# Transposing a branch's normed outputs on VectorE and through DRAM instead of on TensorE

## Chip, cores and metric

The kernel runs on one core of one Trainium2 chip. The metric is device time in microseconds (us) of one execution.

## What is computed

The reference is one layer of a decoder for 256 tokens of 2048 channels. Both of its branches read one input projection.

```python
def hybrid_mixer(h, w_in, ...):
    z = h @ w_in                       # one combined projection
    # A: gated delta rule, 8 heads of 128: o = gated_delta_rule(q, k, v, beta, g)
    oa = rms_norm(o, gdn_norm_w) * silu(zg)
    # B: block-sparse attention, 8 heads of 128 (256 tokens are one causal block)
    ob = moba_attention(mq, mk, mv) * silu(zm)
    y = sigmoid(ga) * (oa @ w_branch_a) + sigmoid(gb) * (ob @ w_branch_b)
    return y @ w_out
```

Only the part on `oa` is changed: its way from the normed and gated outputs (tokens on the partitions) to the operand of `oa @ w_branch_a` (channels on the partitions).

## The kernel before

**Precision.** Every large product is made of fp32r halves. `split` (L249 to L258) takes a block of weights as it came from DRAM (`raw_x`): ScalarE casts the upper half `hi_x` (L256), VectorE subtracts to get the lower half `lo_x` (L257). TensorE multiplies hi by hi, hi by lo and lo by hi. Weights of the input projection come in reads of 1 MB, two for a product; each read is split in two pieces of 128x1024, so that a product has the pieces `x_0_0`, `x_0_1`, `x_1_0`, `x_1_1`. There are three buffers for such a pair (`wspl`), and from some point a fourth, so a cast waits until TensorE has left an earlier piece.

**Order.** TensorE's instructions are pinned in program order by `mm` (L166) and `tr` (L169). Other engines' instructions get their places by a scheduler of the framework, except where `pin` (L164) fixes one. The large products follow the list `ORDER` (L47): `q0 mv0 zg0 q1 kq2 kq3 zg1 v0 v1 v2 ga0 zm0 zm1 mv1 v3 mk0 mk1 mk2 mk3 ga1 ga2 ua0 ua1`, then what is written behind it. Of these `mk3` is the last pair of attention heads (its query product `mq`, then its key product `mk`), `ga1` the next projection, `ua0` and `ua1` the branch products that need what is changed here. Small work is written as Python generators in queues (`gq`, `vq`, `mq`, `aq`, `bq`, `sq`, `zq` and others). `tick` (L159) advances each queue after a step of a large product; the numbers that a generator yields are the ticks that it waits.

**The delta rule's end.** `solve` (L1058) makes the outputs of 8 heads for two halves of 128 tokens. `normed` (L1075) normalizes and gates half `t` into an SBUF tile `oz_t` (128 tokens x 1024 channels, L1106). `prepare` (L876) then starts three 1 MB reads of branch weights on POOL's queue (`tq_g` twice, `tq_z` once, L862) and gives VectorE four sums of them (L870, 128x1024 each) and POOL one more read that accumulates (L873).

**The turn and its sums.** After all heads were attended, `turned_outputs` (L1122) transposes 16 tiles of 128x128 on TensorE (L1130) into four PSUM tiles `ot`; the list `held` stops the queues of the solver and of attention while it runs. `halved` (L1118) reads a PSUM tile twice with the norm's weight `gn` as scale: ScalarE writes the upper half of `oaT`, VectorE the lower. Then four sums of the quarters of `oa` are made, which the seven-product scheme of the branch product (`seven`, L916, a Strassen-like scheme) needs beside the quarters. They are made in PSUM, with copies of one operand to SBUF (`oa_f`) by ScalarE ahead, and halved into `oas`.

**The way through DRAM.** `moved` (L778) writes 32x32 blocks, which VectorE has transposed inside (STREAM_TRANSPOSE), to DRAM (L783) and reads them back in another order (L784), which completes a transpose. It serves attention's probabilities (`pT_d`, 384 KB, written on ScalarE's DMA queue) and the gates (`zm_d`, 256 KB, `turned_gate`, L1253, written on POOL's queue). Reads are on POOL's queue.

**Attention around the change.** `attention` (L1262) makes `mq` and `mk` of two heads; `halves` (L528) adds the two column halves of each head's product into `y_mk`: ScalarE copies one (L531), VectorE adds the other (L532); then VectorE multiplies by `rrow` (L1269). `attend` (L1190) waits for that.

Of the kernel before, what the change touches and what calls it, by code (L numbers as in the profile page):

```python
# [8 lines left out]
F32 = mybir.dt.float32  # L9
F32R = mybir.dt.float32r  # L10
BF16 = mybir.dt.bfloat16
AF = mybir.ActivationFunctionType
ALU = mybir.AluOpType
AX = mybir.AxisListType

P = 128
# [23 lines left out]
A_WAIT2 = 1.5  # L40
A_WAIT3 = 5
A_WAIT4 = 1
G_WAIT = (4, 5)

# [48 lines left out]
def hybrid_layer(  # L95
# [15 lines left out]
    nc = tc.nc  # L111
# [35 lines left out]
    def aux_tile(name):  # L147
        return aux.tile([P, 512], F32, tag="aux", name=name)
# [5 lines left out]

    extra = []

    held = []

    def tick():  # L159
        after[0] -= 0.5  # L160
        for q in (gq, vq, mq, *(() if held else (aq, bq)), *extra):
            q.tick()

    pin = tc.keep_in_program_order  # L164
# [4 lines left out]
    def tr(*args):  # L169
        return pin(nc.tensor.transpose(*args))  # L170
# [608 lines left out]
    def moved(blocks, back, name, writer=nc.gpsimd):  # L779

        n = blocks.shape[1] // 4
        d = dram.tile([4, P, n], F32, name=f"{name}_d")
        pin(writer.dma_start(d.rearrange("i (r j) x -> (i r) (j x)", j=4), blocks))  # L783
        pin(nc.gpsimd.dma_start(back.rearrange("p (i x) -> p i x", i=4), d.rearrange("i k x -> k i x")))  # L784
# [70 lines left out]
    def block(w, c, h, x):  # L855

        return w[h * 512 : (h + 1) * 512, (c + x) * 512 : (c + x + 1) * 512].rearrange("(k p) c -> p k c", p=P)

    def fetch(tq, w, c, order):

        for i in order:
            nc.gpsimd.dma_start(tq[i], block(w, c, *((0, 0), (1, 1), (0, 1))[i]))  # L862

    def weight_sums(tq, w, c, wait):

# [192 lines left out]
    def solve():  # L1058
        oT = big.tile([P, H, 2 * S], F32R, tag="u1", name="oaT")
        oaT[0] = oT  # L1060
        def step(t, which):
            for g in range(2):
                ps = aux_tile(f"sv_{t}_{which}_{g}")
                p3 = ps.rearrange("p (h e) -> p h e", e=P)
                for hh in range(4):
                    h = g * 4 + hh
                    o_ = slice(hh * P, (hh + 1) * P)
                    w = inv[t][:, h, :] if which == 0 else sl(h)[:, P : 2 * P]
                    mm(ps[:, o_], w, vt(0 if which else t, h), start=True, stop=True)
                if which == 0:  # L1070
                    nc.scalar.copy(gvt[g][:, t], p3)
                else:
                    nc.vector.tensor_tensor(gvt[g][:, 1], gvt[g][:, 1], p3, op=ALU.subtract)

        def normed(t, oz):  # L1075

            pso = [aux_tile(f"so_{t}_{g}") for g in range(2)]
            for g, ps in enumerate(pso):
                for hh in range(4):
                    h = g * 4 + hh  # L1080
                    o_ = slice(hh * P, (hh + 1) * P)
                    if t == 0:
                        mm(ps[:, o_], sl(h)[:, 2 * P : 3 * P], vt(0, h), start=True, stop=True)
                    else:
                        mm(ps[:, o_], sl(h)[:, 3 * P : 4 * P], vt(0, h), start=True, stop=False)
                        mm(ps[:, o_], sl(h)[:, 5 * P : 6 * P], vt(1, h), start=False, stop=True)
            for g, ps in enumerate(pso):
                for hh in range(4):
                    h = g * 4 + hh
                    jq = wk.tile([P, P], BF16, tag="jq", name=f"jo_{t}_{h}")  # L1090
                    nc.scalar.activation(
                        jq, ps[:, hh * P : (hh + 1) * P], AF.Square, accum_out=ssoo[:, t, h : h + 1]
                    )
                yield 0.5
            nc.vector.tensor_scalar(
                fo[:, t, :], ssq[:, t, :], EPS, EPS * P, op0=ALU.add, op1=ALU.mult
            )
            nc.vector.scalar_tensor_tensor(
                fo[:, t, :], ssoo[:, t, :], 1.0 / P, fo[:, t, :], op0=ALU.mult, op1=ALU.add
            )  # L1100
            nc.scalar.activation(fo[:, t, :], fo[:, t, :], AF.Sqrt)
            nc.vector.reciprocal(fo[:, t, :], fo[:, t, :])
            for g in range(2):
                for hh in range(4):
                    h = g * 4 + hh
                    nc.vector.scalar_tensor_tensor(  # L1106
                        oz[:, g, hh, :],
                        pso[g][:, hh * P : (hh + 1) * P],
                        fo[:, t, h : h + 1],
                        zg()[:, t, h * P : (h + 1) * P],  # L1110
                        op0=ALU.mult,
                        op1=ALU.mult,
                    )
                yield 0.5

        gn = pcol[:, NTAP * NCV : NTAP * NCV + 1]

        def halved(hi, lo, p3):  # L1118
            nc.scalar.activation(hi, p3, AF.Copy, scale=gn)
            nc.vector.scalar_tensor_tensor(lo, p3, gn, hi.bitcast(F32), op0=ALU.mult, op1=ALU.subtract)  # L1120

        def turned_outputs(ozs):  # L1122


            a = {}
            for t in (1, 0):
                for g in range(2):
                    pt = aux_tile(f"ot_{t}_{g}")
                    for hh in range(4):
                        tr(pt[:, hh * P : (hh + 1) * P], ozs[t][:, g, hh, :], ident)  # L1130
                    a[t, g] = pt.rearrange("p (h n) -> p h n", n=P)
            for t in (1, 0):
                for g in range(2):
                    ks = slice(4 * g, 4 * g + 4)
                    halved(oT[:, ks, t * P : (t + 1) * P], oT[:, ks, S + t * P : S + (t + 1) * P], a[t, g])
                yield 1
            oa_f = big.tile([P, 2, 4, P], F32, tag="tv", name="oa_f")
            x, y = (oa_f[:, i] for i in range(2))
            nc.scalar.copy(x, a[1, 1])
            nc.vector.tensor_tensor(a[1, 1], a[1, 0], x, op=ALU.subtract)  # L1140
            nc.scalar.copy(y, a[0, 0])
            nc.vector.tensor_tensor(a[0, 0], a[1, 1], y, op=ALU.subtract)
            nc.scalar.copy(x, a[0, 0])
            yield 1
            nc.vector.tensor_tensor(a[0, 1], a[0, 1], x, op=ALU.add)
            nc.vector.tensor_tensor(a[1, 0], y, a[1, 0], op=ALU.subtract)
            yield 1
            sums = [None] * 4
            for i, o, tag in ((0, (1, 1), "tt"), (1, (0, 0), "tw"), (3, (0, 1), None), (2, (1, 0), "tv")):
                if tag:  # L1150
                    tl = big.tile([P, 2, 4, P], F32R, tag=tag, name=f"oas_{i}")
                    sums[i] = tl[:, 0], tl[:, 1]
                else:
                    sums[i] = [wk.tile([P, 4, P], F32R, tag="s", name=f"oas_{i}_{n}") for n in ("hi", "lo")]
                halved(*sums[i], a[o])
                yield 1
            oas.extend(sums)

        while vq.items or v_left[0]:
            yield 1  # L1160
        for t, which in ((0, 0), (0, 1), (1, 0)):
            step(t, which)
            yield SV_WAIT
        ozs = [big.tile([P, 2, HG, P], F32, tag=tg, name=f"oz_{t}") for t, tg in enumerate(("tv", "tw"))]
        for t in range(NT):
            yield from normed(t, ozs[t])

        obs.append(big.tile([P, H, 2 * S], F32R, tag="g0", name="obT"))
        tg = big.tile([P, 2, 4, 512], F32, tag="g1", name="tq_g")
        tz = big.tile([P, 4, 512], F32, tag="z2", name="tq_z")  # L1170
        tq = tg[:, 0], tg[:, 1], tz
        prepare(tq, wa, 0, (0, 2, 1))
        yield OS_WAIT
        while attended[0] < H:
            yield 0.5
        held.append(True)
        yield from turned_outputs(ozs)
        held.pop()

    mv = big.tile([P, NT, GW], F32, tag="z1", name="mv")  # L1180

    def attention_values(c):
        pts = proj_n(w_in, CMV + c * 512, hT, KT, f"mv{c}")
        for t in range(NT):
            nc.scalar.activation(mv[:, t, c * 512 : (c + 1) * 512], pts[t], AF.Copy, scale=rstd[:, t : t + 1])


    attended = [0]
# [62 lines left out]
    extra.append(zq)  # L1251

    def turned_gate(p):  # L1253
        yield G_WAIT[p > 0]
        blocks = ga_[:, 2, p % 2]
        to = blocks.rearrange("p (i m t r) -> p t m i r", i=4, m=2, t=NT)
        x = zm()[:, p]
        for t in range(NT):
            pin(nc.vector.transpose(to[:, t], x[:, t].rearrange("p (m c i) -> p m i c", m=2, i=4)))
        moved(blocks, x.rearrange("p t x -> p (t x)"), f"zm_{p}")  # L1260
# [303 lines left out]
```

## Time and profile before

| | |
|---|---|
| median of 3 runs | 758.12 us (757.39 to 758.29) |
| profiled execution, its own time | 757.3 us |
| its span in the trace | 755.6 us |
| mean granted TensorE clock | 0.997 of full speed |
| bytes read from and written to DRAM | 166.39 MB, 6.82 MB |

The profile is of one execution. Its span runs from the first to the last recorded instruction, its own time is 1.7 us longer. PE is TensorE's matrix products, PEld its weight loads (beside the products), DVE VectorE, ACT ScalarE, POOL GpSimd, SP SyncE. A transpose on TensorE is listed as a MATMUL by `ident`. Matrix products overlap: each is listed with its whole duration of 0.4 us, while the next starts 0.23 us later. What a step costs TensorE is therefore read from the distance of starts. Busy times of an engine add up its instructions; an idle time in brackets stands ahead of the instruction that ended it, with what released it.

### The profile page before, as it was taken

Reading aid. Unit: us, or ns where it says so; the run is one execution under the profiler, and the core shown is the slowest. Engines: PE = TensorE matmul, PEld = TensorE weight load, DVE = VectorE, ACT = ScalarE, POOL = GpSimd, SP = SyncE. Lnnn points to the kernel's source line nnn. Section 1 sums busy time; section 2 is a strip of 40 time slices with the busy share of each in tenths; the row PEclk is TensorE's granted clock in tenths of the full one; section 3 lists DMA queues with packets and bytes.
Section 4 is the critical chain, followed back from the end, with each engine's and each line's share of the span. In section 5 each row is a group of like instructions: output and inputs, shape, how many; then the busy total and the mean of one; then the engine's idle time right before and its main releaser. Section 6 shows DMA issues by size and latency. Waiting matters only on the chain.

```text
span 755.6 us, 10416 instructions
## 1 busy us (share of the span) xinstructions
PE 746.3 (99%) x3858; PEld 636.6 (84%) x3858; DVE 597.6 (79%) x963; ACT 456.0 (60%) x693; POOL 65.3 (9%) x97
## 2 busy tenths in 40 slices
PE   9999999999999999999999999999999999999996
PEld 7898988899888888888998888887888888888885
DVE  6877779986988999877568886788796778789864
ACT  6776666667655655455556485557555655765741
POOL 1000201112000000022011100101000101000000
PEclk9999999999999999999999999999999999999998
DMA  9586576458676657698267975998988887987862
GB/s 303 187 259 204 171 234 181 139 149 247 199 248 199 204 182 207 180 273 282 75 190 293 294 240 175 282 326 237 351 235 285 240 265 214 355 258 210 268 250 111
DMA packets 102680, 173.88 MB, mean 230 GB/s; under 512 B 3941, under 2 KB 49702, under 8 KB 102118
## 3 DMA queue, kind: packets, MB, share of 16 engines
q1 hardware_dynamic: 89094, 134.83, 54.6%
q0 software_dynamic: 12496, 36.19, 17.3%
q10 hardware_dynamic: 1040, 2.20, 0.8%
q8 instruction: 30, 0.49, 0.2%
q14 instruction: 20, 0.16, 0.1%
HBM read 166.39 MB, written 6.82 MB: 229 GB/s over the span
## 4 chain that ended last, share of the span: by engine, by line
PE 96%; DVE 2%; ACT 1%; DMA 0%; issue 0%; DVEq 0%; ACTq 0%
PE a_gb L167 12%; PE a_ga L167 11%; PE a_y L167 9%; PE a_ub L167 7%; PE a_zg L167 6%; PE a_k L167 6%; PE a_q L167 6%; PE a_v L167 6%; PE a_mv L167 6%; PE a_zm L167 6%; PE a_mk L167 6%; PE a_mq L167 5%; PE a_ua L167 4%; PE s L167 1%; PE so L167 1%; PE sv L167 1%
## 5 line engine op out<-in xcount | busy, mean ns | idle before, releaser
L167 PE MATMUL a_gb<-hi_gb,hT 128*128 128x512 f32 x256 | 81.1, 391 | 0.0
L167 PE MATMUL a_ga<-hi_ga,hT 128*128 128x512 f32 x256 | 80.9, 391 | 0.0
L167 PEld LDWEIGHTS a_gb<-hi_gb,hT 128*128 128x128 f32 x256 | 48.0, 188 | 10.6
L167 PEld LDWEIGHTS a_ga<-hi_ga,hT 128*128 128x128 f32 x256 | 48.0, 188 | 10.1
L256 ACT CAST hi_ga<-raw_ga 128x1024 fp32r<-128x1024 f32 x32 | 33.6, 1053 | 29.1 <-PE a_ga L167 19.2
L257 DVE TENSOR_TENSOR lo_ga<-raw_ga,hi_ga 128x1024 fp32r<-128x1024 f32 x32 | 39.0, 1222 | 14.5 <-ACT hi_ga L256 14.2
L167 PE MATMUL a_gb<-lo_gb,hT 128*128 128x512 f32 x128 | 50.2, 392 | 0.1
L167 PE MATMUL a_ga<-lo_ga,hT 128*128 128x512 f32 x128 | 49.9, 390 | 0.0
L256 ACT CAST hi_gb<-raw_gb 128x1024 fp32r<-128x1024 f32 x32 | 33.6, 1052 | 25.2 <-PE a_gb L167 13.6
L257 DVE TENSOR_TENSOR lo_gb<-raw_gb,hi_gb 128x1024 fp32r<-128x1024 f32 x32 | 39.1, 1223 | 10.6 <-ACT hi_gb L256 10.3
L167 PE MATMUL a_zg<-hi_zg,hT 128*128 128x348 f32 (+1 forms) x192 | 46.7, 322 | 0.0
L167 PE MATMUL a_mq<-hT,hi_mq 128*128 128x512 f32 x128 | 41.3, 404 | 0.0
L167 PE MATMUL a_mk<-hT,hi_mk 128*128 128x512 f32 x128 | 40.4, 397 | 0.0
L167 PE MATMUL a_q<-hT,hi_q 128*128 128x512 f32 x128 | 40.2, 395 | 0.0
L167 PE MATMUL a_v<-hT,hi_v 128*128 128x512 f32 x128 | 40.2, 395 | 0.0
L167 PE MATMUL a_mv<-hi_mv,hT 128*128 128x512 f32 x128 | 39.9, 391 | 0.0
L167 PE MATMUL a_zm<-hi_zm,hT 128*128 128x512 f32 x128 | 39.5, 389 | 0.0
L167 PE MATMUL a_k<-hT,hi_k 128*128 128x512 f32 (+1 forms) x129 | 38.2, 396 | 0.1
L167 PEld LDWEIGHTS a_zg<-hi_zg,hT 128*128 128x128 f32 x192 | 33.5, 188 | 0.1
L256 ACT CAST hi_mq<-raw_mq 128x1024 fp32r<-128x1024 f32 x16 | 16.8, 1051 | 24.0 <-PE a_mk L167 11.1
L167 PE MATMUL a_zg<-lo_zg,hT 128*128 128x348 f32 (+1 forms) x96 | 30.9, 322 | 0.0
L256 ACT CAST hi_zg<-raw_zg 128x696 fp32r<-128x696 f32 (+1 forms) x24 | 18.5, 772 | 19.1 <-PE a_zg L167 9.0
(467 smaller groups left out, 2029.3 us busy)
## 6 DMA issues: line engine op xcount, KB each, us to landing
raw_ga<-in_w_in_dram SPq DMA_DIRECT2D x16, 1024.0 KB, 5.1
raw_gb<-in_w_in_dram SPq DMA_DIRECT2D x16, 1024.0 KB, 6.1
raw_y<-in_w_out_dram SPq DMA_DIRECT2D x14, 1024.0 KB, 8.0
raw_q<-in_w_in_dram SPq DMA_DIRECT2D x8, 1024.0 KB, 5.5
raw_mv<-in_w_in_dram SPq DMA_DIRECT2D x8, 1024.0 KB, 5.0
raw_v<-in_w_in_dram SPq DMA_DIRECT2D x8, 1024.0 KB, 5.5
raw_zm<-in_w_in_dram SPq DMA_DIRECT2D x8, 1024.0 KB, 5.0
raw_mq<-in_w_in_dram SPq DMA_DIRECT2D x8, 1024.0 KB, 5.9
```

What stands on the lines that cost most here:

```text
L167: return pin(nc.tensor.matmul(*args, **kwargs))
L256: nc.scalar.copy(hi, raw)
L257: nc.vector.tensor_tensor(lo, raw, hi.bitcast(F32), op=ALU.subtract)
```

## The change

1. **VectorE transposes.** As soon as `oz_t` of a half is made, `turned(t, oz)` transposes its 32x32 blocks on VectorE (two STREAM_TRANSPOSE of 128x512 for each half, pinned) into `ot_t`, and `moved` writes them to DRAM (512 KB, ScalarE's queue) and reads them back (POOL's queue) into `backs[t]`, which is free space of the tile `ga`. TensorE's 16 transposes go.
2. **Norm weight.** ScalarE multiplies each `backs[t]` (128x1024) by `gn` in place. `halved` then is a cast and a subtraction without a scale.
3. **Sums.** The four sums are made in SBUF in place by VectorE (four subtractions and additions of 128x512, no copies by ScalarE).
4. **Order.** `turned_outputs` no longer waits until all heads were attended; only the last sum to be halved does. `held` goes, so the solver's and attention's queues are not stopped. The sums are halved in the order 0, 1, 2, 3 (before 0, 1, 3, 2), with half a tick between the halves of `oaT`.
5. **Pins.** The three reads of branch weights are pinned in program order (behind the reads of `ot`) where `oas` is still empty.
6. **The gates.** `G_WAIT` goes from (4, 5) to (4, 5, 5, 7): the last pair's gate is turned two ticks later, in a tile of its own (`spare`).

```diff
-G_WAIT = (4, 5)
+G_WAIT = (4, 5, 5, 7)
...
-        for q in (gq, vq, mq, *(() if held else (aq, bq)), *extra):
+        for q in (gq, vq, mq, aq, bq, *extra):
...
         for i in order:
-            nc.gpsimd.dma_start(tq[i], block(w, c, *((0, 0), (1, 1), (0, 1))[i]))
+            sent = nc.gpsimd.dma_start(tq[i], block(w, c, *((0, 0), (1, 1), (0, 1))[i]))
+            if not oas:
+                pin(sent)
...
         def halved(hi, lo, p3):
-            nc.scalar.activation(hi, p3, AF.Copy, scale=gn)
-            nc.vector.scalar_tensor_tensor(lo, p3, gn, hi.bitcast(F32), op0=ALU.mult, op1=ALU.subtract)
+            hi, lo = (x.rearrange("p h (i y) -> p h i y", i=4) for x in (hi, lo))
+            nc.scalar.copy(hi, p3)
+            nc.vector.tensor_tensor(lo, p3, hi.bitcast(F32), op=ALU.subtract)
+
+        backs = [ga_[:, 1 + t].rearrange("p t n -> p (t n)") for t in range(NT)]
+
+        def turned(t, oz):
+            blocks = big.tile([P, H * P], F32, tag=("tt", "tv")[t], name=f"ot_{t}")
+            to = blocks.rearrange("p (j h y) -> p j h y", j=4, h=H)
+            for g in range(2):
+                hs = slice(g * HG, (g + 1) * HG)
+                pin(nc.vector.transpose(to[:, :, hs], oz[:, g].rearrange("p h (r j) -> p j h r", j=4)))
+            moved(blocks, backs[t], f"ot_{t}", nc.scalar)
 
-        def turned_outputs(ozs):
+        def turned_outputs():
             a = {}
-            for t in (1, 0):
+            for t in range(NT):
+                pin(nc.scalar.activation(backs[t], backs[t], AF.Copy, scale=gn))
...
-                        tr(pt[:, hh * P : (hh + 1) * P], ozs[t][:, g, hh, :], ident)
...
-            nc.scalar.copy(x, a[1, 1])
-            nc.vector.tensor_tensor(a[1, 1], a[1, 0], x, op=ALU.subtract)
-            nc.scalar.copy(y, a[0, 0])
-            nc.vector.tensor_tensor(a[0, 0], a[1, 1], y, op=ALU.subtract)
-            nc.scalar.copy(x, a[0, 0])
+            nc.vector.tensor_tensor(a[1, 1], a[1, 0], a[1, 1], op=ALU.subtract)
+            nc.vector.tensor_tensor(a[1, 0], a[0, 0], a[1, 0], op=ALU.subtract)
...
-        while attended[0] < H:
-            yield 0.5
-        held.append(True)
-        yield from turned_outputs(ozs)
-        held.pop()
+        yield from turned_outputs()
```

Three places show how the rows move. First ScalarE at the last key product `mk`; `hi_mk_i_j` are the upper halves of its weights. Before:

```order
L256 CAST hi_mk_0_1_4176<-raw_mk_0_4143 128x1024
L783 DMA pT_d<-ga 128x768
L256 CAST hi_mk_1_0_4198<-raw_mk_1_4196 128x1024
L256 CAST hi_mk_1_1_4219<-raw_mk_1_4196 128x1024
L256 CAST hi_ga_0_0_4252<-raw_ga_0_4250 128x1024
```

and with the change:

```order
L254 CAST hi_mk_0_1_4187<-raw_mk_0_4155 128x1024
L781 DMA pT_d<-ga 128x768
L1138 ACTIVATE ga<-ga,pcol 128x1024 x2
L1120 CAST oaT<-ga 128x4x128 x3
L254 CAST hi_mk_1_0_4213<-raw_mk_1_4211 128x1024
L1120 CAST oaT<-ga 128x4x128
L254 CAST hi_mk_1_1_4243<-raw_mk_1_4211 128x1024
```

Both multiplications by `gn` and three of the four casts of `oaT` stand between two halves of the product's weights.

Second VectorE, a little later, up to the first lower half of `ga1` (`lo_ga_0_0`). Before:

```order
L257 TENSOR_TENSOR lo_mk_1_0_4199<-raw_mk_1_4196,hi_mk_1_0_4198 128x1024
L870 TENSOR_TENSOR tq_g<-tq_g,tq_z 128x1024
L257 TENSOR_TENSOR lo_mk_1_1_4220<-raw_mk_1_4196,hi_mk_1_1_4219 128x1024
L870 TENSOR_TENSOR tq_g<-tq_g,tq_z 128x1024
L257 TENSOR_TENSOR lo_ga_0_0_4253<-raw_ga_0_4250,hi_ga_0_0_4252 128x1024
L870 TENSOR_TENSOR tq_g<-tq_g 128x1024
L532 TENSOR_TENSOR y_mk_4240<-a_mk_0_4141,y_mk_4240 128x256
```

and with the change, from `lo_mk_1_1` on the second piece (the first ends with the rows that now stand ahead of it):

```order
L870 TENSOR_TENSOR tq_g<-tq_g,tq_z 128x1024
L1147 TENSOR_TENSOR ga<-ga 128x4x4x32
L255 TENSOR_TENSOR lo_mk_1_1_4244<-raw_mk_1_4211,hi_mk_1_1_4243 128x1024
```

```order
L870 TENSOR_TENSOR tq_g<-tq_g,tq_z 128x1024
L1150 TENSOR_TENSOR ga<-ga 128x4x4x32
L530 TENSOR_TENSOR y_mk_4266<-a_mk_0_4153,y_mk_4266 128x256
L1151 TENSOR_TENSOR ga<-ga 128x4x4x32
L530 TENSOR_TENSOR y_mk_4269<-a_mk_1_4154,y_mk_4269 128x256
L1274 TENSOR_TENSOR y_mk_4266<-y_mk_4266,rrow 128x256
L1274 TENSOR_TENSOR y_mk_4269<-y_mk_4269,rrow 128x256
L255 TENSOR_TENSOR lo_ga_0_0_4279<-raw_ga_0_4276,hi_ga_0_0_4278 128x1024
```

`lo_ga_0_0` moves from ahead of the first head's `y_mk` to behind the second head's. The four sums of `oa` (`ga<-ga`) stand among these rows.

Third POOL, which issues the reads. Before the three fetches came first:

```order
L862 DMA tq_g<-in_w_branch_a_dram 128x4x512 x2
L862 DMA tq_z<-in_w_branch_a_dram 128x4x512
L784 DMA pT_4159<-pT_d 128x4x192
L783 DMA zm_d<-ga 128x512
L784 DMA zm<-zm_d 128x4x128
L873 DMA tq_z<-in_w_branch_a_dram 128x4x512
```

and with the change they follow the reads of both halves of `ot`:

```order
L782 DMA ga<-ot_d 128x4x256 x2
L860 DMA tq_g<-in_w_branch_a_dram 128x4x512
L860 DMA tq_z<-in_w_branch_a_dram 128x4x512
L860 DMA tq_g<-in_w_branch_a_dram 128x4x512
L782 DMA pT_4171<-pT_d 128x4x192
L781 DMA zm_d<-ga 128x512
```

`tq_z` now goes ahead of the second `tq_g`. On SP nothing moves. On TensorE the 16 transposes go, and the last pair's attention comes earlier.

## Rows read from the trace of the kernel before

**Rows 1.** The page's shares of the span by engine, and the chain that ended last.

```profile
PE 746.3 (99%) x3858; PEld 636.6 (84%) x3858; DVE 597.6 (79%) x963; ACT 456.0 (60%) x693; POOL 65.3 (9%) x97
...
PE 96%; DVE 2%; ACT 1%; DMA 0%; issue 0%; DVEq 0%; ACTq 0%
```

**Rows 2.** What PE waited for: us in total, times, longest us.

```profile
PE warm L167 <- DVE ones L183: 1.1, 1, 1.1
PE a_mk L167 <- DVE lo_mk L257: 0.3, 1, 0.3
```

**Rows 3.** Windows: span; PE, PEld, DVE, ACT, POOL busy (count); PEclk, DMA share, GB/s.

```profile
397.00:416.00 19.00, 18.69 (x109) 16.14 (x108) 15.58 (x37) 12.46 (x31) 3.54 (x5) 1.00 0.78 290
...
751.00:755.60 4.60, 0.00 (x0) 0.00 (x0) 1.10 (x2) 0.00 (x0) 0.00 (x0) 0.58 0.56 214
```

**Rows 4.** Timeline of PE: start, us, engine, line, operation, out<-in, count [idle before <-releaser].

```profile
438.79 0.39 PE L167 MATMUL a_ga<-lo_ga,hT 128*128 128x512 f32 x1
...
439.47 0.39 PE L167 MATMUL a_ga<-lo_ga,hT 128*128 128x512 f32 x1
...
439.93 1.91 PE L170 MATMUL ot<-ident,oz 128*128 128x128 f32 x16
...
441.90 0.40 PE L167 MATMUL a_ga<-lo_ga,hT 128*128 128x512 f32 x1
```

**Rows 5.** Timeline of PE in the last key product, where its second half of weights begins.

```profile
413.28 0.63 PE L167 MATMUL a_mk<-hT,hi_mk 128*128 128x512 f32 x2
414.22 0.50 PE L167 MATMUL a_mk<-hT,lo_mk 128*128 128x256 f32 x2 [0.31 <-DVE lo_mk L257]
414.56 0.63 PE L167 MATMUL a_mk<-hT,hi_mk 128*128 128x512 f32 x2
...
415.27 0.63 PE L167 MATMUL a_mk<-hT,hi_mk 128*128 128x512 f32 x2
```

**Rows 6.** Timeline of DVE from the last key product to `ga1`.

```profile
411.89 1.16 DVE L1259 STREAM_TRANSPOSE ga<-zm 128x256 f32<-128x256 f32 x2
412.97 2.33 DVE L257 TENSOR_TENSOR lo_mk<-raw_mk,hi_mk 128x1024 fp32r<-128x1024 f32 x2
...
423.56 0.42 DVE L532 TENSOR_TENSOR y_mk<-a_mk,y_mk 128x256 f32<-128x256 f32 x1 [0.78 <-ACT y_mk L531]
423.90 1.22 DVE L257 TENSOR_TENSOR lo_ga<-raw_ga,hi_ga 128x1024 fp32r<-128x1024 f32 x1
```

**Rows 7.** Timeline of ACT in the same stretch.

```profile
410.96 1.05 ACT L256 CAST hi_mk<-raw_mk 128x1024 fp32r<-128x1024 f32 x1
...
411.92 1.05 ACT L256 CAST hi_mk<-raw_mk 128x1024 fp32r<-128x1024 f32 x1
...
422.21 1.05 ACT L256 CAST hi_ga<-raw_ga 128x1024 fp32r<-128x1024 f32 x1 [1.46 <-PE a_mk L167]
423.17 0.36 ACT L531 COPY y_mk<-a_mk 128x256 f32<-128x256 f32 x1
```

**Rows 8.** Groups by line and form: count | busy us, mean ns of one | idle ahead.

```profile
L288 ACT CAST hi_k<-rawf_k 128x512 fp32r<-128x512 f32 x15 | 9.2, 612 | 0.0
...
L1222 DVE STREAM_TRANSPOSE ga<-s 128x384 f32<-128x384 f32 x8 | 6.6, 858 | 1.1 <-ACT s L1217 1.1
```

**Rows 9.** Timeline of POOL from 395 us on: its DMA issues.

```profile
397.47 1.49 POOL L862 DMA_DIRECT2D tq_g<-in_w_branch_a_dram  x2 [3.38 <-ACT jo L1091]
402.02 0.75 POOL L862 DMA_DIRECT2D tq_z<-in_w_branch_a_dram  x1 [3.06 <-DVE oz L1106]
```

**Rows 10.** DMA issues of the whole span: KB each, median us from issue to landing.

```profile
tq_z<-in_w_branch_a_dram POOLq DMA_DIRECT2D x2, 1024.0 KB, 10.2
...
pT_d<-ga ACTq DMA_DIRECT2D x4, 384.0 KB, 3.0
...
pT<-pT_d POOLq DMA_DIRECT2D x4, 384.0 KB, 5.7
```

**Rows 11.** DMA issues from 395 to 412 us alone.

```profile
tq_z<-in_w_branch_a_dram POOLq DMA_DIRECT2D x1, 1024.0 KB, 7.6
```

**Rows 12.** Timeline of PE in the first products of `ga1`.

```profile
422.47 0.40 PE L167 MATMUL a_ga<-lo_ga,hT 128*128 128x512 f32 x1
```

More of the change, by code (lines that the diff above doesn't have):

```diff
@@ L155, in hybrid_layer @@
     extra = []
-    held = []
     def tick():
         after[0] -= 0.5
-        for q in (gq, vq, mq, *(() if held else (aq, bq)), *extra):
+        for q in (gq, vq, mq, aq, bq, *extra):
             q.tick()
@@ L1118, in halved @@
         def halved(hi, lo, p3):
-            nc.scalar.activation(hi, p3, AF.Copy, scale=gn)
-            nc.vector.scalar_tensor_tensor(lo, p3, gn, hi.bitcast(F32), op0=ALU.mult, op1=ALU.subtract)
-        def turned_outputs(ozs):
+            hi, lo = (x.rearrange("p h (i y) -> p h i y", i=4) for x in (hi, lo))
[10 more added lines that the diff above has]
+        def turned_outputs():
             a = {}
-            for t in (1, 0):
+            for t in range(NT):
+                pin(nc.scalar.activation(backs[t], backs[t], AF.Copy, scale=gn))
+                whole_t = backs[t].rearrange("p (i h y) -> p h i y", i=4, h=H)
                 for g in range(2):
-                    pt = aux_tile(f"ot_{t}_{g}")
-                    for hh in range(4):
-                        tr(pt[:, hh * P : (hh + 1) * P], ozs[t][:, g, hh, :], ident)
-                    a[t, g] = pt.rearrange("p (h n) -> p h n", n=P)
-            for t in (1, 0):
+                    a[t, g] = whole_t[:, g * HG : (g + 1) * HG]
+            for t in range(NT):
                 for g in range(2):
@@ L1135, in turned_outputs @@
                     halved(oT[:, ks, t * P : (t + 1) * P], oT[:, ks, S + t * P : S + (t + 1) * P], a[t, g])
-                yield 1
-            oa_f = big.tile([P, 2, 4, P], F32, tag="tv", name="oa_f")
-            x, y = (oa_f[:, i] for i in range(2))
-            nc.scalar.copy(x, a[1, 1])
-            nc.vector.tensor_tensor(a[1, 1], a[1, 0], x, op=ALU.subtract)
-            nc.scalar.copy(y, a[0, 0])
-            nc.vector.tensor_tensor(a[0, 0], a[1, 1], y, op=ALU.subtract)
-            nc.scalar.copy(x, a[0, 0])
+                    yield 0.5
+            nc.vector.tensor_tensor(a[1, 1], a[1, 0], a[1, 1], op=ALU.subtract)
+            nc.vector.tensor_tensor(a[1, 0], a[0, 0], a[1, 0], op=ALU.subtract)
             yield 1
-            nc.vector.tensor_tensor(a[0, 1], a[0, 1], x, op=ALU.add)
-            nc.vector.tensor_tensor(a[1, 0], y, a[1, 0], op=ALU.subtract)
+            nc.vector.tensor_tensor(a[0, 0], a[1, 1], a[0, 0], op=ALU.subtract)
+            nc.vector.tensor_tensor(a[0, 1], a[0, 1], a[0, 0], op=ALU.add)
             yield 1
             sums = [None] * 4
-            for i, o, tag in ((0, (1, 1), "tt"), (1, (0, 0), "tw"), (3, (0, 1), None), (2, (1, 0), "tv")):
+            for i, o, tag in ((0, (1, 1), "tt"), (1, (0, 0), "tw"), (2, (1, 0), "tv"), (3, (0, 1), None)):
+                while not tag and attended[0] < H:
+                    yield 0.5
                 if tag:
@@ L1166, in solve @@
             yield from normed(t, ozs[t])
+            turned(t, ozs[t])
         obs.append(big.tile([P, H, 2 * S], F32R, tag="g0", name="obT"))
@@ L1253, in turned_gate @@
     def turned_gate(p):
-        yield G_WAIT[p > 0]
-        blocks = ga_[:, 2, p % 2]
+        yield G_WAIT[p]
+        blocks = ga_[:, 2, p % 2] if p < 3 else spare[:, : 4 * P]
         to = blocks.rearrange("p (i m t r) -> p t m i r", i=4, m=2, t=NT)
```

## Prediction, made before the change was run

> **What bounds the kernel now.** I read the page's shares first, then what TensorE waited for, then windows, then the timelines of the four engines around the last key product. TensorE is busy for 99% of the span and carries 96% of the chain that ended last [rows 1]. It waited for other engines twice that matter, 1.1 us at the start and 0.3 us for one `lo_mk` [rows 2]. So what leaves TensorE's path is gained, and every wait that the change adds to TensorE is lost, since there is no idle time to take it in. The other engines look roomy: from 397 to 416 us, where the changed part runs, VectorE is busy 15.58 of 19.0 us and ScalarE 12.46, while the DMA share is 0.78 at 290 GB/s [rows 3]. That room is a sum over 19 us. What counts is what stands ahead of the `hi` or `lo` piece that TensorE wants next.
>
> **Gain 1, TensorE's transposes: −1.75 us.** Undisturbed, a `lo_ga` product starts 0.68 us after the one before (438.79 to 439.47). Across the 16 transposes it is 2.43 us (439.47 to 441.90) [rows 4]. The change frees 1.75 us. The Trainium skill (TensorE: Matmul & The Clock Gate, Part 4: PE-mode transpose) gives some 275 ns for one transpose in a kernel; 16 in a row would be 4.4 us, an estimate from that page, and the sum below would be +2.8 us. The row shows that they overlap, so the measured step is used.
>
> **Gain 2, a wait that goes: −0.57 us.** TensorE's step at `lo_mk_0_1` is 1.28 us (413.28 to 414.56) where the next is 0.71 [rows 5]. VectorE did the gate's two transposes (411.89) ahead of that `lo_mk` (412.97) [rows 6]. With the larger `G_WAIT` they stand behind.
>
> **Wait A, ScalarE in front of `hi_mk_1_0`: +1.8 us.** Two multiplications of 128x1024 and three casts of 128x512 now stand between `hi_mk_0_1` and `hi_mk_1_0`. A cast of 128x1024 takes 0.96 us from start to start and 1.05 alone [rows 7]; one of 128x512 takes 0.61 [rows 8], or half of 0.96. That is 3.4 to 3.9 us; I take 3.7. `hi_mk_1_0` then starts at 411.92 + 3.7 = 415.6, ends at 416.7, and its `lo_mk` (1.2 us) at 417.9. TensorE, without the wait of gain 2, wants that at 413.28 + 4 x 0.70 + 0.46 = 416.54. So 1.4 us late.
>
> ScalarE also waits for `ot_1` to come back. POOL was released by the last `oz` at 402.02 [rows 9]. A transpose of 128x384 takes 858 ns [rows 8], so one of 128x512 about 1.1 us by size: 2.2 us for `ot_1`, up to 4.4 if those of `ot_0` are still ahead. The write is bounded by 3.0 us (384 KB) and 4.0 (the same by size), the read by 5.7 (384 KB), twice [rows 10]. The return lies between 402.0 + 2.2 + 3.0 + 5.7 = 412.9 and 402.0 + 4.4 + 4.0 + 5.7 = 416.1. ScalarE comes to the second multiplication at 412.9. I take a return at 413.3, near the lower end because `oz_0` is done well before `oz_1`, and so 0.4 us more: A is 1.8 us, with ends 1.0 (3.4 us and no waiting) and 4.6 (return at 416.1).
>
> **Wait B, VectorE in front of `lo_mk_1_1`: +2.4 us.** The three fetches of branch weights are now pinned behind the read of `ot_1` on POOL's queue. The first ones started at 397.47, 0.75 us each [rows 9]. That read is issued when the write has landed, 407.2 to 410.4; with 408.6, `tq_z` is issued at 410.1. It landed 7.6 us after issue here [rows 11], 10.2 in the median [rows 10], and has 512 KB ahead of it, 1.4 us at 372 GB/s (290 over 0.78 [rows 3]). So it lands between 417.7 and 421.7. VectorE's first sum `tq_g<-tq_g,tq_z` needs it, and behind that sum (1.13 us, as a `lo` step) stand a sum of `oa` (0.6) and `lo_mk_1_1` (1.2): done at 420.6 to 424.6. TensorE wants it 2.8 us after `lo_mk_1_0`, at 419.3 plus A, 421.1. The floor is VectorE's own chain, 0.6 + 1.13 + 0.6 + 1.2 against those 2.8, 0.8 us. Ends 0.8 and 3.6; I take 2.4, a little above the middle, because the two writes and two reads add 2 MB to the stretch with the DMA share of 0.78. Where A is at its upper end, B is at its floor, as the fetch lands during A.
>
> **Wait C, `lo_ga_0_0` behind the last head: +3.6 us.** This one hangs on no transfer. `lo_ga_0_0` now stands behind `y_mk` of the second head. That needs TensorE's last key product and ScalarE's copy, and the copy stands behind `hi_ga_1_0`, whose buffer is free only when TensorE leaves the last piece of `mk`. In the rows this cast starts at 422.21 and the copy at 423.17 [rows 7], VectorE's addition at 423.56 [rows 6]. With 0.34 us each for it and two products by `rrow` and 1.22 for the `lo`, `lo_ga_0_0` is done at 425.8, where TensorE wanted it at 422.47 [rows 12]: 3.3 us. With a sum of `oa` (0.6) in the way it is 3.9. I take 3.6. All times are on the clock of before; A and B move both sides of the difference alike.
>
> **What costs nothing.** VectorE's four transposes (4.4 us in all) and the sums of `oa` fit its idle 3.4 us and the time of the waits A and B [rows 3]; if that cover is gone, they are in the chain of B. ScalarE loses three copies and gets unscaled casts. POOL's two reads are DMA issues of under 0.75 us. The last pair's attention comes earlier, and no one waits for it.
>
> **Sum.** −1.75 − 0.57 + 1.8 + 2.4 + 3.6 = +5.5 us. The profiled execution took 757.3 us and would take 762.8. It lies 0.8 us under the median of the runs shown, so on that median 758.12 + 5.5 = **763.6 us**. The terms' ends give 1.0 + 0.8 + 3.3 − 2.3 = +2.8 and 4.6 + 0.8 + 3.9 − 2.3 = +7.0, so 760.9 to 765.1 us.
>
> **Rivals.**
> *Later transfers.* The writes and reads hinder one another and the read of `ot_1` takes 7.6 us: it is back at 402.0 + 4.4 + 4.0 + 7.6 = 418.0. Then `lo_mk_1_0` ends at 418.0 + 1.0 + 1.8 + 2.25 = 423.05, A is 6.5, B at its floor of 0.8: 6.5 + 0.8 + 3.6 − 2.3 = +8.6, 766.7 us. For it speaks the DMA share of 0.78, against it that 384 KB came back in 5.7 us.
>
> *The clock falls.* In the last window TensorE is idle and the granted clock is 0.58, close to the half level of 1.2 GHz out of 2.4 [rows 3]; here it would stand idle for over 3 us at C. If that lowers the clock and it stays low for one piece of weights, 4 steps of 0.70 us [rows 5] take twice as long: +2.8 more, 766.4 us. Against it speaks that the engine is otherwise busy without a break. The Trainium skill (TensorE: Matmul & The Clock Gate, section "Why this matters for your kernels") says that idle gaps between bursts send the clock back to half; no run here shows it yet for a gap in the middle.
>
> *Other side: the waits are covered and it gets faster.* The place is `ga1`'s start. If ScalarE and VectorE run ahead during TensorE's wait, and `lo_ga_0_0` is ready when wanted, only the gains stay: −2.3 us, 755.8 us. For it speak the idle 3.4 and 6.5 us [rows 3]. Against it stands C: its chain starts with TensorE's last key product, so that nothing can run ahead. The point is where A, B and C together are 2.3 us.
>
> *Nothing to measure.* If `hi_ga_1_0` gets the fourth buffer, the copy starts about 0.96 us earlier and C is 2.4; with A and B gone too, gains and loss balance: 758 us.
>
> The Trainium skill (VectorE: DVE Perf Modes, "Rules for kernel authors") speaks against this change outright: a 128x128 transpose belongs on TensorE where PSUM will do.
>
> **How the numbers follow.** Forecast 0.62, later transfers 0.12, clock 0.15, faster 0.06, nothing 0.05. The range goes from 760.0, just under the lower end of the terms, to 768.0, which takes in both slower rivals. A measurement tells 0.2% (1.5 us) from no change: faster 0.06, same 0.05, slower 0.89.
>
> **What would show it.** In the profile after, TensorE's waits should list `lo_mk` twice (A some 1.8, B some 2.4 us) and `lo_ga` once (3.3 to 3.9), all between 412 and 427 us; `ot` is no more on PE; the step across 440 us is 0.68. If `lo_ga` shows no wait, C was wrong. If A is over 4 us, with ScalarE released by the read of `ot_1`, transfers decide; if products after the wait are at half rate, the clock does.

## The result and the profile after

The changed kernel takes **767.03 us** (median of 4 runs, 766.28 to 767.95), the kernel before 758.2 us in as many runs: a ratio of 1.0118, with a 95% interval of 1.0106 to 1.0130. That is 8.8 us more. It lies inside the range that was given (760.0 to 768.0) and 3.4 us above the predicted time of 763.6, 1.9 us above the upper end of the terms (765.1).

The views of the changed kernel that answer to rows 1 and 2 are the page's shares and what TensorE waited for.

```profile
PE 749.5 (98%) x3842; PEld 637.4 (83%) x3842; DVE 600.8 (79%) x967; ACT 456.3 (60%) x692; POOL 66.7 (9%) x99
```

```profile
PE a_ga L165 <- DVE lo_ga L255: 2.9, 1, 2.9
PE a_mk L165 <- DVE lo_mk L255: 2.7, 3, 1.9
PE warm L165 <- DVE ones L181: 1.1, 1, 1.1
PE a_mk L165 <- ACT hi_mk L254: 0.7, 1, 0.7
```

The 0.3 us of waiting in [rows 2] became 6.3 us, all on pieces of `mk` and `ga1`. TensorE's busy time rose by 3.2 us although 16 transposes went: some products took longer. Both stand in the timeline of PE, which answers to rows 5 and 12.

```profile
413.66 0.63 PE L165 MATMUL a_mk<-hT,hi_mk 128*128 128x512 f32 x2
414.53 0.51 PE L165 MATMUL a_mk<-hT,lo_mk 128*128 128x256 f32 x2 [0.24 <-DVE lo_mk L255]
414.87 0.63 PE L165 MATMUL a_mk<-hT,hi_mk 128*128 128x512 f32 x2
...
416.27 0.63 PE L165 MATMUL a_mk<-hT,hi_mk 128*128 128x512 f32 x2
...
417.86 0.73 PE L165 MATMUL a_mk<-hT,hi_mk 128*128 128x512 f32 x2 [0.73 <-ACT hi_mk L254]
419.12 0.51 PE L165 MATMUL a_mk<-hT,lo_mk 128*128 128x256 f32 x2 [0.53 <-DVE lo_mk L255]
419.46 0.63 PE L165 MATMUL a_mk<-hT,hi_mk 128*128 128x512 f32 x2
...
421.56 0.63 PE L165 MATMUL a_mk<-hT,hi_mk 128*128 128x512 f32 x2
424.07 0.51 PE L165 MATMUL a_mk<-hT,lo_mk 128*128 128x256 f32 x2 [1.88 <-DVE lo_mk L255]
424.41 0.63 PE L165 MATMUL a_mk<-hT,hi_mk 128*128 128x512 f32 x2
...
425.11 1.01 PE L165 MATMUL a_mk<-hT,hi_mk 128*128 128x512 f32 x2
...
427.63 0.63 PE L165 MATMUL a_ga<-hi_ga,hT 128*128 128x512 f32 x1
431.11 0.50 PE L165 MATMUL a_ga<-lo_ga,hT 128*128 128x512 f32 x1 [2.86 <-DVE lo_ga L255]
...
431.91 0.57 PE L165 MATMUL a_ga<-lo_ga,hT 128*128 128x512 f32 x1
...
435.56 0.39 PE L165 MATMUL a_ga<-lo_ga,hT 128*128 128x512 f32 x1
```

An undisturbed step of `mk` (the pair of `hi` products to the next pair) is 0.70 us, one of `ga` (`lo` to the next `lo`) 0.68. Read against these:

| stretch | measured | undisturbed | lost |
|---|---|---|---|
| A, 416.27 to 419.46, two steps | 3.19 | 1.40 | 1.79 |
| B, 421.56 to 424.41, one step | 2.85 | 0.70 | 2.15 |
| slow products, 425.11 to 427.63, two steps | 2.52 | 1.40 | 1.12 |
| C, 427.63 to 431.11, one product | 3.48 | 0.23 | 3.25 |
| slow products, 431.11 to 435.56, four steps | 4.45 | 2.72 | 1.73 |

The sum is 10.0 us. The transposes give 1.6 back. To see this, take the stretch from the last pair's `ms` to the first product of `ua`, in the kernel before:

```profile
431.79 1.47 PE L167 MATMUL ms<-y_mk,y_mq 128*128 128x128 f32 x8
...
471.47 0.48 PE L167 MATMUL a_ua<-hi_ua0p,oaT 128*128 128x512 f32 x1
```

and in the changed one:

```profile
442.13 1.47 PE L165 MATMUL ms<-y_mk,y_mq 128*128 128x128 f32 x8
...
480.18 0.40 PE L165 MATMUL a_ua<-hi_ua0p,oaT 128*128 128x512 f32 x1
```

39.68 us became 38.05. The net loss of 8.4 us agrees with the spans, 755.6 and 764.2, of whose difference 0.4 us is there before the change begins (a `lo_mk` of VectorE starts at 383.87 and 384.25, and the first row of the change, the transposes of `oz_0`, at 393.30).

Why are the products behind B and C slow? The windows of the changed kernel (columns as in rows 3) show it.

```profile
421.00:425.00 4.00, 2.12 (x13) 1.50 (x12) 3.95 (x5) 2.29 (x4) 0.42 (x1) 1.00 0.98 389
425.00:427.60 2.60, 2.60 (x11) 2.22 (x10) 2.60 (x5) 0.39 (x2) 0.56 (x1) 0.53 0.93 278
...
432.00:435.00 3.00, 3.00 (x9) 2.32 (x8) 3.00 (x5) 0.00 (x0) 0.00 (x0) 0.50 1.12 205
```

The granted clock is 0.53 and 0.50 there, the half level of 1.2 GHz, each time behind a stretch in which TensorE was idle. VectorE is busy nearly throughout. Its timeline shows what it did before B and C, and where it stood.

```profile
415.85 1.90 DVE L1121 TENSOR_TENSOR oaT<-ga,oaT 128x512 fp32r<-128x512 f32 x3 [1.37 <-ACT oaT L1120]
417.83 1.23 DVE L255 TENSOR_TENSOR lo_mk<-raw_mk,hi_mk 128x1024 fp32r<-128x1024 f32 x1
...
421.05 1.23 DVE L870 TENSOR_TENSOR tq_g<-tq_g,tq_z 128x1024 f32<-128x1024 f32 x1 [1.39 <-DMA tq_z<-in_w_branch_a_dram]
...
422.80 1.22 DVE L255 TENSOR_TENSOR lo_mk<-raw_mk,hi_mk 128x1024 fp32r<-128x1024 f32 x1
...
428.83 0.42 DVE L530 TENSOR_TENSOR y_mk<-a_mk,y_mk 128x256 f32<-128x256 f32 x1 [0.50 <-ACT y_mk L529]
429.17 0.75 DVE L1274 TENSOR_TENSOR y_mk<-y_mk,rrow 128x256 f32<-128x256 f32 x2
429.84 1.22 DVE L255 TENSOR_TENSOR lo_ga<-raw_ga,hi_ga 128x1024 fp32r<-128x1024 f32 x1
```

It waited 1.37 us for ScalarE (A) and 1.39 us for the fetch of `tq_z` (B); behind that there is one short wait, of 0.50 us, up to `lo_ga`.

### The profile page after: what moved, and what is told of

Read it like the earlier page. It is cut to its first block, busy times and chain, and to the rows that moved or that the text cites. A ratio compares the mean times of both kernels' runs of the same rounds, so it can differ in the third digit from the quotient of the medians.

```text
span 764.2 us, 10397 instructions
## 1 busy us (share of the span) xinstructions
PE 749.5 (98%) x3842; PEld 637.4 (83%) x3842; DVE 600.8 (79%) x967; ACT 456.3 (60%) x692; POOL 66.7 (9%) x99
## 3 DMA queue, kind: packets, MB, share of 16 engines
q10 hardware_dynamic: 1328, 3.25, 1.1%
## 5 line engine op out<-in xcount | busy, mean ns | idle before, releaser
L165 PEld LDWEIGHTS a_mk<-hT,lo_mk 128*128 128x128 f32 x128 | 24.4, 192 | 9.6 <-DVE lo_mk L255 4.0
L165 PEld LDWEIGHTS a_ga<-lo_ga,hT 128*128 128x128 f32 x128 | 24.4, 190 | 8.9 <-DVE lo_ga L255 3.8
```

What stands on the lines that cost most here:

```text
L165: return pin(nc.tensor.matmul(*args, **kwargs))
```

## The experiments

The theory after the result: three waits A, B and C, as in the prediction, and a clock that falls behind B and C. Open were whether the idle time is what lowers the clock, and whether C is a matter of order (`lo_ga_0_0` behind `y_mk`) or of VectorE's backlog, so that it would come out elsewhere in any order.

**e1_fill: is it the idle TensorE that lowers the clock?**

```diff
+    def filling(n):
+        junk = aux_tile(f"junk{n}")
+        for _ in range(n):
+            mm(junk, hT[:, 0, :P], hT[:, 0, : 2 * S], start=True, stop=True)
...
+                if name == "mk6" and kb == 1 and m == 1:
+                    filling(6)
...
+        if p == 3:
+            filling(12)
```

> The change, with 6 and 12 products more on TensorE (128x512, into a PSUM tile that nobody reads) ahead of the last piece of the last mk and ahead of ga1, so that TensorE is busy where it waited for lo_mk_1_1 (B) and lo_ga_0_0 (C). Theory (the three waits are what they are, and the idle TensorE loses its clock behind B and C, 1.1 and 1.7 us): the added products cost nothing, since they run in the gaps, the granted clock stays at 1.00 from 424 to 436 us, the steps behind the waits are 0.70 us, and the time falls by 2.8 us from 767.0 to 764.2. Rival (the slow products behind the waits are slow for another reason, such as operands that come late): steps of 1.25 us stay, time 767.

764.64 us, ratio 1.0086 (1.0073 to 1.0100), 2.4 us less than the changed kernel by the medians. With 18 products more to do, the kernel is faster. Its windows:

```profile
425.00:427.60 2.60, 2.60 (x16) 2.26 (x15) 2.60 (x5) 1.35 (x3) 0.56 (x1) 1.00 0.95 281
427.60:431.00 3.40, 2.83 (x13) 2.04 (x12) 3.40 (x7) 0.83 (x3) 1.87 (x2) 1.00 0.69 198
```

The clock stays at 1.00 (from 431 to 435 us too) where it was 0.53 and 0.50, and the longest wait left, beside the one at the start, is 0.7 us. So the slow products were the clock, and it fell because TensorE was idle. The forecast was 2.8 us less. Between the two profiled executions it is 2.0 (spans 764.2 and 762.2): the slow products' 2.85 us are gone, but the places of B and C take 0.2 us more each (421.42 to 424.47 and 426.57 to 430.25), and the step at `lo_ga_0_1` 0.4 more (432.69 to 433.79).

**e2_unpin: is the pin of the fetches what makes B?**

```diff
-            if not oas:
-                pin(sent)
```

> The change without the pins of the three weight fetches, which go back to ahead of the read of ot_1 on POOL's queue. Theory (the pin alone makes B): B falls from 2.1 to VectorE's own 0.8 us, so that the clock behind it also stays up, 1.3 + 1.1 less, 764.6 us. Rival (the queue is the limit, whichever goes first): the read of ot_1 now stands behind 3 MB of fetches, comes back some 4 to 6 us later than 413, and ScalarE's multiplication holds hi_mk_1_0: A is 6 to 7 us in place of 1.8 and released by the read of ot_d, time 768 to 770.

771.53 us, ratio 1.018 (1.0167 to 1.0194): the rival in the waits, and 1.5 us over its range in time. TensorE's waits:

```profile
PE a_mk L165 <- ACT hi_mk L254: 6.5, 1, 6.5
PE a_ga L165 <- DVE lo_ga L255: 3.2, 1, 3.2
```

B is gone, C stays (3.2 us), and A is 6.5 us: ScalarE holds `hi_mk_1_0` until the read of `ot_1` is back. The cause is not the one that the rival named, the place behind the fetches on POOL's queue. POOL stood idle ahead of that read, until the write of `ot_1` had landed:

```profile
414.57 0.75 POOL L782 DMA_DIRECT2D ga<-ot_d  x1 [9.92 <-DMA ot_d<-ot]
```

That write, issued on ScalarE's queue at 405.64, took 8.9 us beside the fetches, at a DMA share of 1.02; in the changed kernel it took 3.6 (404.90 to 408.46), at 0.69. The read took 6.0 us, 4.3 in the changed kernel. The pin chose the smaller of two evils. Whichever transfers go first, the others' user waits.

**e3_defer: is C the order of `lo_ga_0_0` and `y_mk`?** The last pair's `y_mk` is written 1.5 ticks later in the program.

```diff
-        kTs = [halves(pk[m], f"mk{h + m}") for m in range(2)]
-        for m in range(2):
-            nc.vector.tensor_tensor(kTs[m], kTs[m], rrow, op=ALU.mult)
+        kTs = []
+        def keys_made():
+            if p == 3:
+                yield DEFER
+            kTs.extend(halves(pk[m], f"mk{h + m}") for m in range(2))
+            for m in range(2):
+                nc.vector.tensor_tensor(kTs[m], kTs[m], rrow, op=ALU.mult)
...
+        hq.add(keys_made())
```

> The change, with the last pair's y_mk (copies, additions, products by rrow) written 1.5 ticks later in the program, so that lo_ga_0_0 stands ahead of them on VectorE. Theory (C is a matter of order: lo_ga_0_0 behind y_mk): C of 3.3 us and the slow products behind it, 1.7 us, go; 762.0 us. Rival (C is VectorE's backlog: more work than the stretch has time for, in whatever order): the wait comes back in pieces at lo_ga_0_0, lo_ga_0_1 and lo_ga_1_0, 3 to 4 us in sum; as no piece is as long as C, the clock may stay up behind them: 765 to 767 us.

764.62 us, ratio 1.0091 (1.0077 to 1.0105): the rival again, 0.4 us under its range. The timeline of PE lists the pieces:

```profile
425.56 0.50 PE L166 MATMUL a_mk<-hT,lo_mk 128*128 128x256 f32 x2 [2.24 <-DVE lo_mk L256]
...
430.07 0.50 PE L166 MATMUL a_ga<-lo_ga,hT 128*128 128x512 f32 x1 [1.69 <-DVE lo_ga L256]
...
433.54 0.50 PE L166 MATMUL a_ga<-lo_ga,hT 128*128 128x512 f32 x1 [0.46 <-DVE lo_ga L256]
...
439.20 0.50 PE L166 MATMUL a_ga<-lo_ga,hT 128*128 128x512 f32 x1 [1.30 <-DVE lo_ga L256]
```

The three at `lo_ga` are 3.4 us in sum, against 2.9 at one place before. `lo_ga_0_0` stood ahead of `y_mk`, and it came out no cheaper. TensorE's waits on `mk` and `ga` are even longer in sum, 7.1 us against 6.3; the gain of 2.4 us is the clock, 1.00 all through. So the order is not the whole cause: without it, VectorE's backlog makes TensorE wait as long. It is not nothing either: in the changed kernel VectorE itself stood idle for 0.50 us, waiting for ScalarE's copy, shortly before `lo_ga_0_0` (its timeline above).

**e4_late_unpin: is it the sums and fetches, or the way through DRAM?** The fetches are unpinned, and the wait for all heads stands ahead of the sums again.

```diff
-            if not oas:
-                pin(sent)
...
         yield OS_WAIT
+        while attended[0] < H:
+            yield 0.5
         yield from turned_outputs()
```

> The change without the pins of the fetches, and with the wait for all heads attended back ahead of the multiplications by gn and the sums (they then run in ga1, as before the change; VectorE's transposes and the way through DRAM stay early). Theory (A, B and C all come from the sums and fetches being in front of mk's and ga1's pieces, not from the way through DRAM itself): no wait on TensorE between 412 and 445 us but the one of 0.3 at lo_mk_0_1, the clock stays up, and what is left is the gain of the 16 transposes: 758.2 - 1.75 = 756.4 us. Rival (the added DMA and VectorE work wants its time wherever it stands): new waits in ga1 or ga2 of 1 to 4 us, 757.5 to 760 us.

758.0 us, ratio 1.0003 (0.9994 to 1.0012), in the rival's range. In this kernel part of the sums is computed from other data: they read `backs` after `ga1`'s results have taken that space; the instructions and their times are those of the sums. The long waits are gone, so it is the sums and fetches that make them. But the gain of the transposes does not show: TensorE's list has three small waits on `lo_mk` and `lo_ga`, 0.9 us in sum and the longest 0.4 us, and the products behind each of them start late by some 0.1 us more.

**e5_twait: the backlog tested from its other side.** The four sums of weights come six ticks later.

```diff
-T_WAIT = (5, 4, 4, 4)
+T_WAIT = (11, 4, 4, 4)
```

> The change with the first T_WAIT 11 in place of 5: VectorE's four sums of branch weights (1.13 us each) come six ticks later, out of the stretch from 412 to 432 us, and nobody there waits for the fetch of tq_z. Everything else as changed. Theory (C is VectorE's backlog, made by the work added and by the time that VectorE stood waiting for tq_z): B (2.1 us) and the slow products behind it (1.1) go, C shrinks from 3.3 to 1 to 1.5 us, the clock stays up behind it (1.7), and A stays at 1.8: 767.0 - 2.1 - 1.1 - 2.0 - 1.7 = 760.2 us. Rival (C is only the order of lo_ga_0_0 and y_mk and ScalarE's late copy): B goes, C stays at 3.3 with its slow products: 763.8 us.

768.31 us, ratio 1.0136 (1.0123 to 1.0149): slower, and neither was forecast. TensorE's waits:

```profile
PE po L165 <- DMA pT<-pT_d: 5.8, 1, 5.8
PE a_ga L165 <- DVE lo_ga L255: 1.6, 1, 1.6
```

In the stretch itself B is gone, A is as it was, and the granted clock stays at 1.00. `lo_ga_0_0` is there in time; the wait of 1.6 us is at the next piece, `lo_ga_0_1`. This piece now stands behind `y_mk` of the second head, for which VectorE again waited for ScalarE's copy. TensorE's timeline has the wait, VectorE's what went before:

```profile
429.04 0.50 PE L165 MATMUL a_ga<-lo_ga,hT 128*128 128x512 f32 x1 [1.62 <-DVE lo_ga L255]
```

```profile
426.49 0.42 DVE L530 TENSOR_TENSOR y_mk<-a_mk,y_mk 128x256 f32<-128x256 f32 x1 [0.49 <-ACT y_mk L529]
```

So less work on VectorE shortens the wait at the start of `ga1`, from 2.9 us to 1.6, and does not remove it. And a new wait of 5.8 us stands at the last pair's `po`. The timeline of POOL has it:

```profile
446.62 1.33 POOL L873 DMA_DIRECT2D tq_z<-in_w_branch_a_dram  x1 [14.51 <-DVE tq_g L870]
447.40 1.33 POOL L782 DMA_DIRECT2D pT<-pT_d  x1
```

The accumulating read of `tq_z` waited 14.51 us for VectorE's sums, and the read of `pT` went right behind it. POOL held it back little: it was issued 3.9 us after its write (443.50), 3.5 in the changed kernel. But it landed 14.5 us after its issue, with that 1 MB ahead of it in its queue, where it takes 4.6 us in the changed kernel.

**e6_spread and e8_spread_po: a version without the waits.** In e6 the multiplications, casts and sums of `oa` are spread over more ticks, and the fetches come after the first of them:

```diff
-T_WAIT = (5, 4, 4, 4)
+T_WAIT = (7, 4, 4, 4)
...
-OS_WAIT = 3
+OS_WAIT = 5
+P_WAIT = 2
...
                     halved(oT[:, ks, t * P : (t + 1) * P], oT[:, ks, S + t * P : S + (t + 1) * P], a[t, g])
-                    yield 0.5
+                    yield 1
...
-        prepare(tq, wa, 0, (0, 2, 1))
+        parts = turned_outputs()
         yield OS_WAIT
-        yield from turned_outputs()
+        since = 0
+        for wait in parts:
+            if since is not None and since >= P_WAIT:
+                prepare(tq, wa, 0, (0, 2, 1))
+                since = None
...
```

> The change with its work spread out: OS_WAIT 5 in place of 3 and one tick in place of a half between the halves of oaT (ScalarE's multiplications and casts move behind hi_mk_1_1), the fetches two ticks after these, and the first T_WAIT 7 (sums of weights at the end of ga1). All sums are still made before ga1's results take their space. Theory (all three waits are a matter of too much work in one place): no wait on TensorE over 0.3 us from 412 to 470 us, clock 1.00, and the gain of the 16 transposes (1.6 us across 440 in the profile after) shows: 758 - 1.6 = 756.4 us, below both kernels. Rival (with the sums late, e4 showed no long wait but 0.2 to 0.4 us at several lo pieces, and no gain): such small waits eat the 1.6 us again, 757.4 to 758.3 us.

757.63 us (12 runs, 757.04 to 761.75), ratio 1.0007 (0.9995 to 1.0020): the rival's range. No wait over 0.3 us is left from 412 to 470 us, but one at `ua`:

```profile
472.31 0.50 PE L166 MATMUL a_ua<-lo_ua0p,oaT 128*128 128x512 f32 x1 [0.94 <-DVE lo_ua0p L256]
```

Its chain is on ScalarE: the cast of `hi_ga` ahead of `hi_ua0p` waited for a read, which took 9.3 us (5.0 in the kernel before).

```profile
468.81 1.05 ACT L255 CAST hi_ga<-raw_ga 128x1024 fp32r<-128x1024 f32 x1 [5.18 <-DMA raw_ga<-in_w_in_dram]
```

In the kernel before the same cast waited 0.87 us. The reads of `tq_ua` (1 MB each) went at 454.58 and 456.85 us in e6, as their space was free early, and at 472.02 and 474.30 in the kernel before. e8 holds back the last pair's `po`, which frees that space:

```diff
-        yield A_WAIT3
+        yield A_WAIT3 + (6 if h == H - 2 else 0)
```

> The kernel of e6_spread, with the last pair's attention products (po) six ticks later, so that they stand ahead of ua as in the kernel before. Theory (in e6 the early po set the space of mv and zm free at 454 us, POOL's 2 MB for tq_ua went at once, the read of raw_ga for ga3 came late, and lo_ua0p behind it made TensorE wait 1.6 us at 471): the two tq_ua reads go after 468 us, no wait at ua, time 757.6 - 1.6 = 756.0 us, below both kernels. Rival (the read of raw_ga is late for another reason, or the wait moves on): a wait of over 0.5 us stays between 465 and 480 us, 757 to 758 us.

**756.19 us**, ratio 0.9977 (0.9968 to 0.9986): faster than both kernels, and 1.8 us below the kernel before as measured beside it (757.95). The stretch from the last pair's `ms` to the first product of `ua` is 37.92 us (433.24 to 471.16) where it was 39.68 with the transposes. Beside the one at the start, which all kernels have, TensorE waited twice:

```profile
PE a_mv L166 <- DVE lo_mv L256: 0.5, 1, 0.5
PE a_mk L166 <- DVE lo_mk L256: 0.2, 1, 0.2
```

and VectorE is as busy as it can be, beside a TensorE that never stands still:

```profile
421.00:427.00 6.00, 6.00 (x32) 5.09 (x31) 5.91 (x10) 4.00 (x7) 2.98 (x4) 1.00 0.97 327
427.00:432.00 5.00, 5.00 (x26) 4.22 (x25) 5.00 (x10) 3.36 (x6) 0.00 (x0) 1.00 1.02 410
```

**e7_gwait: was gain 2 there to be had?** The kernel before, with the change's gates alone.

```diff
-G_WAIT = (4, 5)
+G_WAIT = (4, 5, 5, 7)
...
-        yield G_WAIT[p > 0]
-        blocks = ga_[:, 2, p % 2]
+        yield G_WAIT[p]
+        blocks = ga_[:, 2, p % 2] if p < 3 else spare[:, : 4 * P]
```

> The kernel before, with the gates' part of the change alone (G_WAIT (4, 5, 5, 7) and the last gate's blocks in spare). Theory (gain 2 of the prediction was right for the kernel before, and in the changed kernel the four transposes of oz took the place of the gate's): TensorE's step at lo_mk_0_1 falls from 1.28 to 0.71 us, time 757.2 us. Rival (softmax holds that lo_mk anyway): the step stays over 1.1 us, time 757.7 us.

757.35 us, ratio 0.9992 (0.9982 to 1.0001). The time cannot be told from no change, but the trace can: there is no wait left on `lo_mk`, and the two steps there take 1.39 us (413.45 to 414.84).

```profile
413.45 0.63 PE L167 MATMUL a_mk<-hT,hi_mk 128*128 128x512 f32 x2
...
414.84 0.63 PE L167 MATMUL a_mk<-hT,hi_mk 128*128 128x512 f32 x2
```

**e9_osw: are the three waits independent?**

```diff
-OS_WAIT = 3
+OS_WAIT = 5
```

> The change with OS_WAIT 5 in place of 3 and nothing else: ScalarE's multiplications and casts of oaT move behind hi_mk_1_1. Theory (VectorE's backlog; each wait is only where it comes out): A (1.8 us) goes, and its time comes back as longer waits at lo_mk_1_1, lo_ga_0_0 or lo_ga_0_1, 7 us and more in sum with the clock low behind them: 766 to 769 us. Rival (the three waits are independent, each of its own order): A goes and B and C stay as they are: 767.0 - 1.8 = 765.2 us or less.

766.95 us, ratio 1.0121 (1.0107 to 1.0135), as the changed kernel's 1.0118. A is gone, and its time is back at B (3.8 us) and later pieces:

```profile
PE a_mk L165 <- DVE lo_mk L255: 4.1, 2, 3.8
PE a_ga L165 <- DVE lo_ga L255: 2.9, 2, 2.3
```

VectorE's timeline says why: without A's casts it had nothing to do, and the fetch came no sooner.

```profile
420.91 1.23 DVE L870 TENSOR_TENSOR tq_g<-tq_g,tq_z 128x1024 f32<-128x1024 f32 x1 [4.53 <-DMA tq_z<-in_w_branch_a_dram]
```

## Why the prediction was right, and where it fell short

**Gain 1, −1.75: right.** 1.63 us measured, and e8 has it as a gain of the whole kernel (1.8 us).

**Gain 2, −0.57: wrong.** The step at `lo_mk_0_1` is 1.21 us (413.66 to 414.87), as good as unchanged. e7 shows that the gate's transposes caused the wait in the kernel before and that moving them removes it. The step that failed is the sentence that VectorE's four transposes cost nothing: the two of `ot_1` (2.09 us from 402.77) stand ahead of softmax, whose own transposes start at 411.06 in place of 409.72, and `lo_mk_0_1` behind them is as late as before. ScalarE's `hi_mk_0_1`, which that piece needs, came late with softmax too (412.14, done at 413.19, 0.04 us before `lo_mk_0_1` started). That they are the cause is read from the timeline, no run took them away alone.

**A, +1.8: right.** 1.79 us, by the road described, but without the wait for `ot_1`. Its read was issued at 408.46 (forecast 408.6), and ScalarE went from `hi_mk_0_1` into the multiplications at once. It came to them late instead: `hi_mk_0_1` started at 412.14, against 410.96 in [rows 7], as softmax was late (see gain 2). The added work itself was sized well: `hi_mk_1_0` started 4.62 us behind `hi_mk_0_1` where it was 0.96, so 3.66 more against the 3.7 taken. That a late softmax stood in for the 0.4 us put down to `ot_1` is luck. e2 shows that the wait for `ot_1` is there as soon as the read is later.

**B, +2.4: right, 2.15.** `tq_z` was issued at 409.94 and VectorE's sum started when it landed, at 421.05. That is 11.1 us, over the 10.2 taken as the upper row, and at 421.0 inside the landing times given (417.7 to 421.7). The forecast counted 512 KB ahead of `tq_z` in the queue; the order of the change has a `tq_g` of 1 MB between as well, so it was 1.5 MB. That the range held in spite of this is in part luck: the row of 7.6 us also had fetches still under way ahead of it (issued at 397.47, 7.0 us to landing).

**C, +3.6: the size right (3.25, lower end 3.3), the reason half right.** The chain over ScalarE's copy and `y_mk` is in the timeline, but e3 shows that to break it gains nothing in waits. What is behind it is work: VectorE lost 2.8 us waiting in A and B and then had the weights' sums, those of `oa`, the gate's transposes and every `lo` to do. e5 took 4.5 us of it away, and what was left was 1.6 us, on the same chain at the next piece. So chain and backlog stand side by side; no run says what either would cost alone.

**The clock: the step that cost the forecast its accuracy.** It was a rival, priced at +2.8 us for the total of 766.4, with a chance of 0.15. Measured are 1.12 + 1.73 = 2.85 us. That the size agrees is luck: it was priced for one fall, behind C, with four steps twice as long, and there were two falls with less behind each. e1 shows the mechanism. The rule of the Trainium skill that was named there (TensorE: Matmul & The Clock Gate, section "Why this matters for your kernels"), that idle gaps send the clock back to half, agrees with these windows. That some waits did not lower it is told at the end. The chance was too low: the forecast itself put TensorE idle three times within 15 us, and the only row on an idle TensorE said that the clock falls.

With these, the forecast's sum becomes −1.63 − 0.06 + 1.79 + 2.15 + 3.25 + 2.85 = +8.4 us, against 8.8 between the medians.

The rule that speaks against the change (the Trainium skill, VectorE: DVE Perf Modes, "Rules for kernel authors") was borne out for this version of it, not for the idea: the kernel of e8 turns the tiles in the same way and is faster than the one with TensorE's transposes.

## What to carry to other kernels

Where one engine is busy for 99%, moving 1.6 us of work off it pays only if every piece that it wants next stays on time: count, for the engine that takes the work over, what stands ahead of the next piece and what it must wait for, not its idle share over 19 us. When such an engine has a backlog, reordering only moves the wait (e3, e9), and moving the work out of the stretch can move the wait to what is queued behind it (e5); what helps is to spread the work and to look again at each queue (e6, e8). And price an idle TensorE at more than the wait: the products behind it may run at half the clock.

## What was not expected

- **The length of a wait alone does not decide on the clock.** Behind the wait of 1.88 us (B of the changed kernel) the granted clock was 0.53. In e3 a wait of 2.24 us and in e9 one of 2.35 us at `lo_ga` left it at 1.00. Waits of 2.86 us (C), 3.8 (e9) and 5.8 (e5) were all followed by about half the clock. What else goes into it stays open.
- **An earlier release can hurt far away.** In e6 products that ran 17 us earlier set space free, and beside the 2 MB of reads that used it a read that TensorE's next product depended on took 9.3 us in place of 5.0.
- **More work on the busiest engine made the kernel 2.4 us faster** (e1), since it kept the clock up.
